# Hymba step on one Trainium2 core: weight loads issued in the order of their use

## The chip, the core and the metric

The kernel runs on one core of one Trainium2 chip. Five engines matter: TensorE (PE in the profile, its weight loads PEld), VectorE (DVE), ScalarE (ACT), GpSimd (POOL) and SyncE (SP). Each takes its instructions from its own queue, in order, and waits on semaphores for the others. SP computes nothing here: it issues every DMA of the kernel, all 1,546 of them, one behind the other, and a load whose buffer is not free holds all that stand behind it in SP's queue.

The metric is device time in microseconds of one execution. Besides the times of several runs there is one profiled execution with a trace of all instructions.

## The reference

One layer of a hybrid decoder, for 2048 prompt tokens and 32 sample tokens, in float32:

```python
def layer(x, mk, mv, s0, buf, mix_p, g_x, wq_x, wo_x, g_ffn, w_gate, w_up, conv_w, conv_b, w_down):
    m, S, sv = mixer(rmsnorm(x, mix_p[0]), s0, mix_p)
    h = x + m
    h = h + mem_attend(rmsnorm(h, g_x), mk, mv, wq_x, wo_x)
    f, new_buf = conv_ffn(rmsnorm(h, g_ffn), buf, w_gate, w_up, conv_w, conv_b, w_down)
    return h + f, S, new_buf, sv

def conv_ffn(hn, buf, w_gate, w_up, conv_w, conv_b, w_down):
    g = hn @ w_gate
    gp = jnp.concatenate([buf.astype(g.dtype), g], axis=1)
    c = conv_b + sum(conv_w[j] * gp[:, j:j + T] for j in range(CONV_W))
    return (jax.nn.gelu(c) * (hn @ w_up)) @ w_down, gp[:, -(CONV_W - 1):]
```

`mixer` is a gated linear attention (GLA) beside a chunked spatial gate (SGU), between a joint input projection `w_in` (1024 x 2576) and an output projection `w_out`; `mem_attend` is a cross attention over 256 memory tokens; `d_model` is 1024, `d_ff` 2816. The outputs are the hidden states, the states of GLA and of the convolution, the memory's keys and values, and the sample tokens' gate rows.

## The kernel before

**Arithmetic.** A float32 product is made of three PE passes: each operand is split into a part `h` (a copy rounded to the type that PE takes at full rate, by ACT, L85) and the rest `l` (DVE, L86), and `mm3` (L92 to L95) adds h·h, h·l and l·h. The large products with fixed weights go by a seven-product scheme (Strassen's form): its weight operands are three plain quarters A11, A12, A22 and four sums S1 to S4.

**Work.** The prompt goes in four blocks of 512 tokens, `s` = 0 to 3, through input projection, SGU and GLA, output projection, memory attention and FFN. The 32 sample tokens ride along: in the mixer with block 1, their memory attention (`sample_steps`, tiles `w_sq`, `kc`, `vc`) woven into the FFN of block 1, their FFN with block 2. Ahead of block 0 stand the memory's keys and values and the folding of the attention's weights. In the FFN of block 0 the weights are loaded as they are, split, and their split forms written to DRAM (`w7g`, `w7u` plain quarters, `s7g`, `s7u` sums, `wd` the split down weights); blocks 1 to 3 read these.

**Weight tiles.** Two rings in SBUF hold weights. *Raw* tiles (`rp`, 128 x 1024 float32, `NR` = 3 buffers, names `w_...`) take what must still be split. *Weight* tiles (`wp`, `NW` = 10 buffers) take what PE reads: `h_` and `l_` tiles of a split (two per raw tile), or plain tiles that come ready from DRAM. All are 512 KB. The FFN of blocks 1 to 3 takes each gate or up step (`seven_step`, eleven of either, named `wg<block><step>` and `wup<block><step>`) from five loads: A11 and A12 ready (one weight tile each), S2 with S3 raw, S1 with S4 raw (each split into two weight tiles), A22 ready. PE turns between a gate step and an up step, twelve matmuls of 256 columns on a tile quarter at a time. The `down` product reads eight ready tiles (`h_wd`, `l_wd`) for each group of four steps. In the mixer `tm_steps` loads `w_wr1` 0 to 3 as raw tiles; for block 1 some raw tiles are *held*, since the sample tokens use them unsplit (matmuls `t_wr1q`, L745).

**What sets the order.** The program is a list of `Step`s with units (their loads). `run()` walks the list and makes units ahead of their step as long as the two rings have room (`room`, L512): a unit's `load()` makes the raw load, the split and the weight tiles in one go. What the engines run is then set by a list scheduler at build time: it takes an instruction up when its operands and its buffer are free by its own timeline. Raw loads and ready loads have no order between them in this program; a raw load can be placed as soon as one of the raw buffers is free.

```python
def room(live, kind, n, size):
    return not live or made[kind] + n - live[0][0] <= size
```

Activations live in a pool `up` of `NU` = 51 tiles of 128 x 544 (`U`), with a smaller one of 8 (`T_`).

Of the kernel before, what the change touches and what calls it, by code (L numbers as in the profile page):

```python
# [9 lines left out]
F32 = mybir.dt.float32  # L10
# [27 lines left out]
def hymba_step_kernel(  # L38
# [9 lines left out]
    nc = tc.nc  # L48
# [48 lines left out]
    def W(name):  # L97
        return wp.tile([128, 1024], F32R, tag="w", name=name)

    def unit_of(load, ring=2, raws=0, held=False):  # L100
        load.ring, load.raws, load.held, load.until = ring, raws, held, None
        return load

    def raw_tile(name):
        return rp.tile([128, 1024], F32, tag="raw", name=f"w_{name}")

    def wload(w, k0, nk, m0, mw, name):
        t = raw_tile(name).rearrange("p (k m) -> p k m", k=nk)
        nc.sync.dma_start(t, w[k0 * 128:(k0 + nk) * 128, m0:m0 + mw].rearrange("(k p) m -> p k m", p=128))
        return t  # L110

    def wsplit(raw, name):

        hi, lo = (W(f"{x}_{name}").rearrange("p (k m) -> p k m", k=raw.shape[1]) for x in "hl")
        split(hi, lo, raw)
        return hi, lo

    def wunit(*spec):
        return unit_of(lambda: wsplit(wload(*spec), spec[-1]), 2, 1)

    def wraw_unit(*spec):
        return unit_of(lambda: wload(*spec), 0, 1, True)
# [12 lines left out]
    def wkeep(dst, *spec):  # L135

        def load():
            out = wsplit(wload(*spec), spec[-1])
# [3 lines left out]
        return unit_of(load, 2, 1)  # L142

# [6 lines left out]
    def seven_tile(src, name):  # L150

        def load():
            t = W(name).rearrange("p (x k m) -> p x k m", x=2, k=4)
            nc.sync.dma_start(t.bitcast(F32), src)
            return t
        return unit_of(load, 1)

# [43 lines left out]
            out[first], out[second] = (h[:, lo_], l[:, lo_]), (h[:, hi_], l[:, hi_])  # L201
        return out

    def sums_load(src, k, name):
        t = raw_tile(name)
        nc.sync.dma_start(t, src)
        return wsplit(t.rearrange("p (k m) -> p k m", k=k), name)

    def seven_step(plain, sums, get_xs, H, outs, use, name, early=False, then=None):

# [5 lines left out]
        def unit(nm):  # L216
            if nm in PLAIN:
                return seven_tile(plain[:, PLAIN.index(nm)], f"{name}{nm}")
            i = SUMS.index(nm)
            return unit_of(lambda: sums_load(sums[:, i:i + 2].rearrange("p s k m -> p (s k m)"), 8,  # L220
                                             f"{name}{nm}"), 2, 1)

        def hold(nm, w):
            if nm in PLAIN:
# [151 lines left out]
    for l in range(7):  # L376
        half = 1 << l
        n = 64 // half
# [101 lines left out]

    class Step:
        def __init__(self, fn, units=(), parts=None):
            self.fn, self.units = fn, [u if callable(u) else wunit(*u) for u in units]
            self.parts = parts or [self]

    def weave(main, *sides):
# [17 lines left out]
    def run(steps):  # L504


        steps = [p for st in steps for p in st.parts]
        index = {st: i for i, st in enumerate(steps)}
        queue = [(i, u) for i, st in enumerate(steps) for u in st.units]
        ready = {}  # L510
        ring, raws = [], []
        made = {"ring": 0, "raws": 0}  # L512
        at = 0

        def room(live, kind, n, size):
            return not live or made[kind] + n - live[0][0] <= size

        for i, st in enumerate(steps):
            now[0] = i
            flush(i - 1)  # L520
            for live in (ring, raws):
                while live and live[0][1] < i:
                    live.pop(0)
            while at < len(queue):
                j, u = queue[at]
                if not (room(ring, "ring", u.ring, NW) and room(raws, "raws", u.raws, NR)):
                    break
                until = index[u.until] if u.until else j
                if u.ring:
                    ring.append((made["ring"], j if u.held else until))  # L530
                if u.held:
                    raws.append((made["raws"], until))
                ready.setdefault(j, []).append(u())
                made["ring"] += u.ring
                made["raws"] += u.raws
                at += 1
            assert len(ready.get(i, ())) == len(st.units)
            st.fn(*ready.pop(i, []))
# [174 lines left out]
        return [(0, 272), (272, 272)] if sample else [(0, 512)]  # L713

    def wmake(w, k0, nk, m0, mw, name, dst, u):
        return unit_of(lambda: seven_make(wload(w, k0, nk, m0, mw, name), *dst, u, name), 2, 1)

    def fm_step(w, m0, get_xs, sample, evac, name, make=None):

# [15 lines left out]
    def tm_steps(w, m0, get_xs, sample, evac, name):  # L735


        ps = {}
        held = []

        def spread(j):
            if j == 1:
                ps["q"] = mps(f"t_{name}q")
            for k, raw in reversed(held):
                pe.matmul(ps["q"][hr[k % 4]], sxg[:, k * NS:(k + 1) * NS], raw, start=j == 1, stop=j == 3)  # L745
            held.clear()
            if j == 3:
                ps["t"] = T_(f"t_{name}t")
                act.activation(ps["t"][:, :512], ps["q"], AF.Copy)

        def fn(j, wu):
            xs = get_xs()
            raw, wh, wl = wu
            if sample:
                held.extend((2 * j + kk, raw[:, kk]) for kk in range(2))
                if j % 2:
                    spread(j)
            for c in range(4):
                cs = slice(c * 128, (c + 1) * 128)
                if j == 0:  # L760
                    ps[c] = acc(f"t_{name}{c}")
                for kk in range(2):
                    k = 2 * j + kk
                    mm3(ps[c], xs[k][0][:, cs], xs[k][1][:, cs], wh[:, kk], wl[:, kk], k == 0, k == 7)
                if j == 3:
                    evac(ps[c], c, 128)
            if sample and j == 3:
                ps[4] = mps(f"t_{name}4")
                pe.matmul(ps[4][:NS], sum4, ps["t"][:, :512], start=True, stop=True)
                evac(ps[4][:NS], 4, NS)  # L770

        def unit(j):
            def load():
                raw = wload(w, 2 * j, 2, m0, 512, f"{name}{j}")
                return raw, *wsplit(raw, f"{name}{j}")
            return unit_of(load, 2, 1, sample)
# [549 lines left out]
    def attention_steps(B):  # L1326
# [17 lines left out]
        def score(i, nm):  # L1344


            plain, sums = q7d[i]

            def fn(wu):
                wh, wl = wu  # L1350
                if nm == "A11":
                    B.p[i], B.ps = [None] * 4, {}
                fresh = nm in ("A11", "S1", "A12", "A22")
                if fresh:
                    B.ps[CHAIN[nm]] = acc(f"sc{s}{i}{nm}")
# [16 lines left out]
            def load():  # L1372
                return sums_load(sums[:, SUMS.index(nm)].rearrange("p k m -> p (k m)"), 4, f"qk{s}{i}{nm}")

            return Step(fn, [wready(plain[:, PLAIN.index(nm)], f"qk{s}{i}{nm}") if nm in PLAIN else unit_of(load, 2, 1)])

        def soften(i, j):

# [491 lines left out]
```

## Time and profile before

| | before |
|---|---|
| median of 3 runs | 2878.17 us (2877.86 to 2878.55) |
| profiled execution | 2877.25 us |
| its span, first to last instruction | 2875.5 us |
| mean granted clock of PE in it | 0.992 |
| moved by DMA | 592.04 MB, 205 GB/s over the span |

The page splits the span into 40 slices; each digit is a busy share in tenths, the last row the GB/s of a slice.

```profile
PE   8999999999999999999999999999999999999998
DMA  8766579999822255776885216566665324566664
GB/s 278 223 202 205 183 256 300 332 317 310 279 88 76 83 161 193 288 260 228 289 296 174 81 59 227 179 226 231 220 229 177 91 70 155 188 237 227 232 230 154
```

One slice is 71.9 us. PE is busy in all of them; the transfers are at their height in slices 7 to 11, the FFN of block 0, in which the weights are both read and written back in split form. The slices with little transfer are the mixers of blocks 1 to 3. Views used below: PE's *waits* (who waited, for which tile, total us, times, longest), *windows* (busy time and granted clock between two moments) and SP's *timeline* (when a DMA was issued). A time on SP's timeline is that of the issue; the data land later.

### The profile page before, as it was taken

To read this page: it belongs to the slowest core of one execution; us is meant where nothing else is said; L and a number is where in the kernel's file an instruction comes from. 1 tells how busy PE (TensorE), PEld (TensorE's weight loads), DVE (VectorE), ACT (ScalarE), POOL (GpSimd) and SP (SyncE) were. 2 spreads that over 40 slices of the span, in tenths; PEclk is the share of its full clock that TensorE was granted. 3 is DMA by queue.
4 is the path that set the end of the run, shared out by engine and by line. 5 is a ranking of instruction groups with operands and counts; after the bars stand their busy time and mean duration, and the time that the engine had idled before them with its cause. 6 is when DMAs were issued, how large, how long until landed. Compare 5 with 4: busy or idle time off the path is not lost.

```text
span 2875.5 us, 46693 instructions
## 1 busy us (share of the span) xinstructions
PE 2807.7 (98%) x17894; PEld 2482.3 (86%) x17894; DVE 1835.4 (64%) x3054; ACT 1216.2 (42%) x2185; POOL 562.7 (20%) x638
## 2 busy tenths in 40 slices
PE   8999999999999999999999999999999999999998
PEld 8788888888888798888888879899999888889987
DVE  6577767666747776555545777755556777654554
ACT  5545544233453354333333545533333545433333
POOL 2001212111110312222310121323221121121221
PEclk9999999999999999999999999999999999999999
DMA  8766579999822255776885216566665324566664
GB/s 278 223 202 205 183 256 300 332 317 310 279 88 76 83 161 193 288 260 228 289 296 174 81 59 227 179 226 231 220 229 177 91 70 155 188 237 227 232 230 154
DMA packets 348213, 592.04 MB, mean 206 GB/s; under 512 B 25610, under 2 KB 225388, under 8 KB 347990
## 3 DMA queue, kind: packets, MB, share of 16 engines
q1 hardware_dynamic: 347990, 589.06, 61.3%
q8 instruction: 141, 2.31, 0.3%
q14 instruction: 82, 0.67, 0.1%
HBM read 473.09 MB, written 115.87 MB: 205 GB/s over the span
## 4 chain that ended last, share of the span: by engine, by line
PE 83%; DMA 6%; DVE 5%; ACT 3%; issue 2%; POOL 1%; SPq 0%; POOLq 0%; ACTq 0%; DVEq 0%
PE d L95 6%; PE d L93 6%; PE d L94 6%; PE a_wx L95 2%; PE a_wx L94 2%; PE a_wx L93 2%; PE s L1082 2%; PE a_wg L95 1%; PE a_wup L95 1%; PE a_wup L93 1%; PE a_wg L93 1%; PE a_wg L94 1%; PE a_wup L94 1%; PE a_wu L95 1%; PE a_wu L93 1%
## 5 line engine op out<-in xcount | busy, mean ns | idle before, releaser
L93 PE MATMUL d<-acth,h_wd 128*128 128x512 f32 (+1 forms) x864 | 305.0, 354 | 0.9 <-DMA h_wd<-wd 0.9
L95 PE MATMUL d<-acth,l_wd 128*128 128x512 f32 (+1 forms) x864 | 302.6, 351 | 1.3 <-DMA l_wd<-wd 1.3
L94 PE MATMUL d<-actl,h_wd 128*128 128x512 f32 (+1 forms) x864 | 303.2, 351 | 0.0
L1719 DVE TENSOR_TENSOR h<-d,h 128x512 f32<-128x512 f32 (+1 forms) x232 | 135.0, 584 | 151.9 <-PE d L95 151.6
L95 PEld LDWEIGHTS d<-acth,l_wd 128*128 128x128 f32 x864 | 162.4, 188 | 24.1 <-DMA l_wd<-wd 2.1
L93 PEld LDWEIGHTS d<-acth,h_wd 128*128 128x128 f32 x864 | 162.4, 188 | 22.7 <-PE sop L1429 1.4
L94 PEld LDWEIGHTS d<-actl,h_wd 128*128 128x128 f32 x864 | 162.7, 188 | 20.5 <-issue 0.6
L1614 POOL TENSOR_TENSOR c<-c,bc_f 128x512 f32<-128x512 f32 (+1 forms) x88 | 128.0, 1460 | 160.8 <-ACT c L1613 159.8
L1636 POOL TENSOR_TENSOR c<-q,c 128x512 f32<-128x512 f32 (+1 forms) x33 | 48.5, 1470 | 412.7 <-DVE q L298 289.5
L1604 ACT ACTIVATE c<-g,colsb 128x512 f32<-128x512 f32 x88 | 70.7, 811 | 129.7 <-DVE g L1565 76.7
L93 PE MATMUL a_wo<-ch,h_wo 128*128 128x512 f32 (+1 forms) x320 | 115.3, 369 | 1.0 <-ACT ch L89 0.9
L94 PE MATMUL a_wo<-cl,h_wo 128*128 128x512 f32 (+1 forms) x320 | 113.3, 356 | 0.0
L95 PE MATMUL a_wo<-ch,l_wo 128*128 128x512 f32 (+1 forms) x320 | 113.1, 356 | 0.0
L85 ACT ACTIVATE acth<-c 128x512 fp32r<-128x512 f32 (+1 forms) x88 | 55.9, 637 | 121.4 <-POOL c L1636 49.5
L95 PE MATMUL a_wx<-pTh,l_wx 128*128 128x512 f32 x256 | 100.7, 394 | 0.0
L1601 POOL COPY carry<-g 128x2 f32<-128x2 f32 x88 | 36.3, 413 | 329.2 <-DVE g L1565 263.6
L94 PE MATMUL a_wx<-pTl,h_wx 128*128 128x512 f32 x256 | 100.3, 393 | 0.0
L93 PE MATMUL a_wx<-pTh,h_wx 128*128 128x512 f32 x256 | 98.8, 394 | 0.0
L86 DVE TENSOR_TENSOR actl<-c,acth 128x512 fp32r<-128x512 f32 (+1 forms) x88 | 65.0, 740 | 48.5 <-ACT acth L85 47.8
L1613 ACT ACTIVATE c<-c 128x512 f32<-128x512 f32 (+1 forms) x88 | 55.3, 636 | 78.5 <-DVE c L1606 72.3
L1605 DVE SCALAR_TENSOR_TENSOR c<-g,colsb,c 128x512 f32<-128x512 f32 x88 | 69.6, 795 | 16.3 <-ACT c L1604 16.3
L1606 DVE SCALAR_TENSOR_TENSOR c<-g,colsb,c 128x512 f32<-128x512 f32 x88 | 75.0, 856 | 1.3
(4117 smaller groups left out, 9542.5 us busy)
## 6 DMA issues: line engine op xcount, KB each, us to landing
h_wd<-wd SPq DMA_DIRECT2D x66, 512.0 KB
l_wd<-wd SPq DMA_DIRECT2D x66, 512.0 KB
w_wo<-in_w_out_dram SPq DMA_DIRECT2D x32, 512.0 KB
h_wx<-vod SPq DMA_DIRECT2D x32, 512.0 KB
l_wx<-vod SPq DMA_DIRECT2D x32, 512.0 KB
w_wg<-in_w_gate_dram SPq DMA_DIRECT2D x22, 512.0 KB
w_wup<-in_w_up_dram SPq DMA_DIRECT2D x22, 512.0 KB
w_wd<-in_w_down_dram SPq DMA_DIRECT2D x22, 512.0 KB
```

The source lines that it names most:

```text
L85: act.activation(hi, src, AF.Copy)
L86: (lo_eng or dve).tensor_tensor(lo, src, hi.bitcast(F32), ALU.subtract)
L93: pe.matmul(ps, wh, xh, start=first, stop=False, skip_group_check=again)
L94: pe.matmul(ps, wh, xl, start=False, stop=False, skip_group_check=again)
L95: pe.matmul(ps, wl, xh, start=False, stop=last, skip_group_check=again)
L1082: pe.matmul(ps3[:, :, c * 64:(c + 1) * 64], kl[:, c * 128:(c + 1) * 128], kr3[:, :, c * 64:(c + 1) * 64], start=True, stop=True)
L1604: act.activation(c[:, :SB], g[:, 2:SB + 2], AF.Identity, bias=cb, scale=w2)
L1605: dve.scalar_tensor_tensor(c[:, :SB], g[:, 1:SB + 1], w1, c[:, :SB], ALU.mult, ALU.add)
L1606: dve.scalar_tensor_tensor(c[:, :SB], g[:, 0:SB], w0, c[:, :SB], ALU.mult, ALU.add)
L1613: act.activation(c[:, :T], c[:, :T], AF.Gelu_apprx_tanh)
L1614: pool.tensor_tensor(c[:, :T], c[:, :T], B.fbc[:, :T], ALU.mult)
L1719: dve.tensor_tensor(B.h[m + mm][:, cs], ps[:, :cw], B.h[m + mm][:, cs], ALU.add)
```

## The change

A unit now has two parts: `raw`, which makes the raw load, and `make`, which splits it. `fetch()` issues every load of a weight and ties it to the one before it, so that SP issues weight loads in the order in which the program makes them (an order for the scheduler, without a semaphore). `run()` calls `fetched(done + 2)` ahead of each split: the raw tile of this split and that of the next one are loaded, no more. Raw tiles number four, at 4 KB of each partition, and activation tiles 49 instead of 51.

```diff
-NU, NT, NW, NR = 51, 8, 10, 3
+NU, NT, NW, NR = 49, 8, 10, 4
...
+    in_turn = mybir.DependencyInfo(mybir.DependencyClass.NoSync, mybir.DependencyReason.DATA)
+    before = []
+
+    def fetch(dst, src):
+        ins = nc.sync.dma_start(dst, src).ins
+        if before:
+            tc.add_manual_dep(ins, before.pop(), in_turn, reason="weights in turn")
+        before.append(ins.name)
...
-        nc.sync.dma_start(t, w[k0 * 128:(k0 + nk) * 128, m0:m0 + mw].rearrange("(k p) m -> p k m", p=128))
+        fetch(t, w[k0 * 128:(k0 + nk) * 128, m0:m0 + mw].rearrange("(k p) m -> p k m", p=128))
...
     def wunit(*spec):
-        return unit_of(lambda: wsplit(wload(*spec), spec[-1]), 2, 1)
+        return unit_of(lambda raw: wsplit(raw, spec[-1]), 2, lambda: wload(*spec))
...
-                nc.sync.dma_start(t.bitcast(F32), src[:, x])
+                fetch(t.bitcast(F32), src[:, x])
...
-        ready = {}
-        ring, raws = [], []
-        made = {"ring": 0, "raws": 0}
-        at = 0
+        raws = [(i, u) for i, u in queue if u.raw]
+        ready, ring, held, loaded = {}, [], [], {}
+        made = at = nraw = done = 0
+
+        def fetched(upto):
+            nonlocal nraw
+            while nraw < min(upto, len(raws)):
+                i, u = raws[nraw]
+                if held and nraw - held[0][0] >= NR:
+                    break
+                if u.held:
+                    held.append((nraw, index[u.until] if u.until else i))
+                loaded[id(u)] = u.raw()
+                nraw += 1
...
-                if not (room(ring, "ring", u.ring, NW) and room(raws, "raws", u.raws, NR)):
+                if ring and made + u.ring - ring[0][0] > NW:
                     break
+                if u.raw:
+                    fetched(done + 2)
+                    if id(u) not in loaded:
+                        break
+                    done += 1
...
-                ready.setdefault(j, []).append(u())
+                ready.setdefault(j, []).append(u.make(*([loaded.pop(id(u))] if u.raw else [])))
```

The other edits of the diff give each kind of unit (`wkeep`, `wmake`, `sums_load`, the units of `tm_steps` and of the query product) the same two parts. The instructions are the same in number and kind. Line numbers behind L97 shift by up to 17, and every weight load now stands at L109, in `fetch`. Three places of the order that the build gives:

SP, in the mixer of block 1, before: the loads of the weights `w_wr11` to `w_wr13`, a row of the gate's constants, stores of sample results (`svo`, `so`), two tiles of cached keys, and the output projection's first tile.

```order
L109 DMA w_wr11_9018<-in_w_in_dram 128x2x512
L109 DMA w_wr12_9024<-in_w_in_dram 128x2x512
L944 DMA gsgub_9035<-in_g_sgu_dram 32x512
L946 DMA out_8_dram<-svo_9036 32x512
L1198 DMA out_6_dram<-so00_8876 128x4x128
L1462 DMA kc000_12075<-in_cache_mem_k_dram 128x512
L1198 DMA out_6_dram<-so01_8891 128x4x128
L1462 DMA kc001_12077<-in_cache_mem_k_dram 128x512
L109 DMA w_wr13_9404<-in_w_in_dram 128x2x512
L109 DMA w_wo140_9410<-in_w_out_dram 128x4x256
```

The same place now:

```order
L109 DMA w_wr11_8741<-in_w_in_dram 128x2x512
L109 DMA w_wr12_9020<-in_w_in_dram 128x2x512
L109 DMA w_wr13_9026<-in_w_in_dram 128x2x512
L963 DMA gsgub_9037<-in_g_sgu_dram 32x512
L965 DMA out_8_dram<-svo_9038 32x512
L1217 DMA out_6_dram<-so00_8878 128x4x128
```

The load of `w_wr13` has moved six places ahead, directly behind `w_wr12`.

SP, in the FFN of block 3, around the ready tiles of gate step 8 (`wg38A11`, `wg38A12`), before:

```order
L154 DMA wup37A12_27688<-w7u7_205 128x1024
L206 DMA w_wg38S1_27907<-s7g8_208 128x1024
L206 DMA w_wup38S2_28098<-s7u8_210 128x1024
L154 DMA wup37A22_27785<-w7u7_205 128x1024
L154 DMA wg38A11_27816<-w7g8_207 128x1024
L154 DMA wg38A12_27818<-w7g8_207 128x1024
L206 DMA w_wup38S1_28132<-s7u8_210 128x1024
```

and now:

```order
L109 DMA wup37A12_27690<-w7u7_205 128x1024
L109 DMA w_wup37S1_27710<-s7u7_206 128x1024
L109 DMA w_wg38S2_27781<-s7g8_208 128x1024
L109 DMA wup37A22_27787<-w7u7_205 128x1024
L109 DMA wg38A11_27818<-w7g8_207 128x1024
L109 DMA wg38A12_27820<-w7g8_207 128x1024
L109 DMA w_wg38S1_27838<-s7g8_208 128x1024
L109 DMA w_wup38S2_27909<-s7u8_210 128x1024
```

`w_wg38S1` and `w_wup38S2` stood ahead of `wg38A11`; they now stand behind `wg38A12`. On ACT, at the same place, the splits (`h_`) and the copies of accumulators (`q`, `g`) and the convolution (`c`) before:

```order
L85 ACTIVATE h_wg38S_27838<-w_wg38S_27836 128x1024
L1604 ACTIVATE c_27802<-g_27690,colsb 128x512
L85 ACTIVATE h_wg38S_27909<-w_wg38S_27907 128x1024
L1604 ACTIVATE c_27810<-g_27692,colsb 128x512
L292 ACTIVATE q_27820<-a_wup37x 128x256
L292 ACTIVATE q_27821<-a_wup37z 128x256
```

and now:

```order
L85 ACTIVATE h_wg38S_27840<-w_wg38S_27781 128x1024
L1621 ACTIVATE c_27804<-g_27692,colsb 128x512
L1621 ACTIVATE c_27812<-g_27694,colsb 128x512
L304 ACTIVATE q_27822<-a_wup37x 128x256
L304 ACTIVATE q_27823<-a_wup37z 128x256
L304 ACTIVATE g_27944<-a_wg38x 128x256
L1630 ACTIVATE c_27804<-c_27804 128x512
L85 ACTIVATE h_wg38S_27911<-w_wg38S_27838 128x1024
```

The second split has moved behind the other rows shown.

SP, in the FFN of block 1, where the sample attention's query weights (`w_sq20`, `w_sq21`, raw and held) come between two steps, before:

```order
L206 DMA w_wup11S1_11735<-s7u1_182 128x1024
L109 DMA w_sq20_11754<-in_wq_x_dram 128x4x256
L109 DMA w_sq21_11756<-in_wq_x_dram 128x4x256
L154 DMA wup11A22_11741<-w7u1_181 128x1024
L154 DMA wg12A11_11758<-w7g2_183 128x1024
L154 DMA wg12A12_11760<-w7g2_183 128x1024
L206 DMA w_wg12S2_11778<-s7g2_184 128x1024
L206 DMA w_wg12S1_11877<-s7g2_184 128x1024
```

and now:

```order
L109 DMA w_wup11S1_11633<-s7u1_182 128x1024
L109 DMA wup11A22_11708<-w7u1_181 128x1024
L109 DMA w_sq20_11743<-in_wq_x_dram 128x4x256
L109 DMA w_sq21_11756<-in_wq_x_dram 128x4x256
L109 DMA w_wg12S2_11758<-s7g2_184 128x1024
L109 DMA wg12A11_11760<-w7g2_183 128x1024
L109 DMA wg12A12_11762<-w7g2_183 128x1024
L109 DMA w_wg12S1_11780<-s7g2_184 128x1024
```

`wup11A22` went ahead of the two sample tiles, `w_wg12S2` ahead of `wg12A11`.

More of the change, by code (lines that the diff above doesn't have):

```diff
@@ L98, in W, with unit_of @@
         return wp.tile([128, 1024], F32R, tag="w", name=name)
-    def unit_of(load, ring=2, raws=0, held=False):
-        load.ring, load.raws, load.held, load.until = ring, raws, held, None
-        return load
+    def unit_of(make, ring=2, raw=None, held=False):
+        return NS_(make=make, ring=ring, raw=raw, held=held, until=None)
+    in_turn = mybir.DependencyInfo(mybir.DependencyClass.NoSync, mybir.DependencyReason.DATA)
[5 more added lines that the diff above has]
+        before.append(ins.name)
     def raw_tile(name):
@@ L135, in wkeep, with make @@
     def wkeep(dst, *spec):
-        def load():
-            out = wsplit(wload(*spec), spec[-1])
+        def make(raw):
+            out = wsplit(raw, spec[-1])
             for x, t in enumerate(out):
@@ L141, in load @@
             return out
-        return unit_of(load, 2, 1)
+        return unit_of(make, 2, lambda: wload(*spec))
     PLAIN, SUMS = ("A11", "A12", "A22"), ("S1", "S4", "S2", "S3")
@@ L153, in load @@
             t = W(name).rearrange("p (x k m) -> p x k m", x=2, k=4)
-            nc.sync.dma_start(t.bitcast(F32), src)
+            fetch(t.bitcast(F32), src)
             return t
@@ L202, in seven_tokens, with sums_unit, raw @@
         return out
[L204 to L207, printed above, removed]
+    def sums_unit(src, k, name):
+        def raw():
+            t = raw_tile(name)
+            fetch(t, src)
+            return t.rearrange("p (k m) -> p k m", k=k)
+        return unit_of(lambda raw: wsplit(raw, name), 2, raw)
     def seven_step(plain, sums, get_xs, H, outs, use, name, early=False, then=None):
@@ L482, in __init__ @@
         def __init__(self, fn, units=(), parts=None):
-            self.fn, self.units = fn, [u if callable(u) else wunit(*u) for u in units]
+            self.fn, self.units = fn, [wunit(*u) if isinstance(u, tuple) else u for u in units]
             self.parts = parts or [self]
@@ L520, in run @@
             flush(i - 1)
-            for live in (ring, raws):
+            for live in (ring, held):
                 while live and live[0][1] < i:
@@ L525, in run @@
                 j, u = queue[at]
-                if not (room(ring, "ring", u.ring, NW) and room(raws, "raws", u.raws, NR)):
+                if ring and made + u.ring - ring[0][0] > NW:
                     break
-                until = index[u.until] if u.until else j
-                if u.ring:
-                    ring.append((made["ring"], j if u.held else until))
-                if u.held:
-                    raws.append((made["raws"], until))
-                ready.setdefault(j, []).append(u())
-                made["ring"] += u.ring
-                made["raws"] += u.raws
+                if u.raw:
[3 more added lines that the diff above has]
+                    done += 1
+                if u.ring:
+                    ring.append((made, index[u.until] if u.until and not u.held else j))
+                ready.setdefault(j, []).append(u.make(*([loaded.pop(id(u))] if u.raw else [])))
+                made += u.ring
                 at += 1
@@ L772, in unit @@
         def unit(j):
[L773 to L776, printed above, removed]
+            return unit_of(lambda raw: (raw, *wsplit(raw, f"{name}{j}")), 2,
+                           lambda: wload(w, 2 * j, 2, m0, 512, f"{name}{j}"), sample)
         out = [Step(lambda wu, j=j: fn(j, wu), [unit(j)]) for j in range(4)]
@@ L1370, in fn @@
                     soften(i, o)
-            def load():
-                return sums_load(sums[:, SUMS.index(nm)].rearrange("p k m -> p (k m)"), 4, f"qk{s}{i}{nm}")
-            return Step(fn, [wready(plain[:, PLAIN.index(nm)], f"qk{s}{i}{nm}") if nm in PLAIN else unit_of(load, 2, 1)])
+            return Step(fn, [wready(plain[:, PLAIN.index(nm)], f"qk{s}{i}{nm}") if nm in PLAIN else
+                             sums_unit(sums[:, SUMS.index(nm)].rearrange("p k m -> p (k m)"), 4, f"qk{s}{i}{nm}")])
         def soften(i, j):
```

9 lines of the change are left out of this document (3 added, 6 removed).

## The prediction

> **What bounds the kernel now.** I read the page first. Its busy line and its chain say that TensorE sets the time almost alone.
>
> ```profile
> span 2875.5 us, 46693 instructions
> PE 2807.7 (98%) x17894; PEld 2482.3 (86%) x17894; DVE 1835.4 (64%) x3054; ACT 1216.2 (42%) x2185; POOL 562.7 (20%) x638
> PE 83%; DMA 6%; DVE 5%; ACT 3%; issue 2%; POOL 1%; SPq 0%; POOLq 0%; ACTq 0%; DVEq 0%
> ```
>
> PE works for 2807.7 of 2875.5 us. The change alters no matmul, so all that an order of loads can give back lies in the other 67.8 us, and in the time that matmuls run at half clock. The second view is therefore that of PE's waits: who waited, for what, total us, times, longest. These are the waits that the change can touch, and one for a split, which gives a price below.
>
> ```profile
> PE t_wr1q L745 <- DMA w_wr<-in_w_in_dram: 4.0, 1, 4.0
> PE a_wup15x L93 <- ACT q L292: 2.6, 1, 2.6
> PE a_wg32x L93 <- DMA wg32A<-w7g: 2.5, 1, 2.5
> PE a_wg16x L93 <- DMA wg16A<-w7g: 2.3, 1, 2.3
> PE a_wg12x L93 <- DVE c L1605: 2.2, 1, 2.2
> PE a_wg38x L93 <- DMA wg38A<-w7g: 2.1, 1, 2.1
> PE a_wg310x L93 <- DVE nct L1780: 1.6, 1, 1.6
> PE mkp L93 <- ACT h_wk L85: 1.5, 1, 1.5
> PE a_wg18x L93 <- DMA wg18A<-w7g: 1.4, 1, 1.4
> PE d L95 <- DMA l_wd<-wd: 1.3, 2, 0.8
> PE a_wg34x L93 <- DMA wg34A<-w7g: 1.2, 1, 1.2
> PE d L93 <- DMA h_wd<-wd: 0.9, 1, 0.9
> ```
>
> For a_wg12x and a_wg310x the profile names the last of several semaphores; the matmuls there are the first on a plain tile, like the others, so I read them as waits for that tile (nct and c read accumulators that were done before). The waits for loads sum to 4.0+2.5+2.3+2.2+2.1+1.6+1.4+1.3+1.2+0.9 = 19.5 us, with a_wup15x, which follows wg16's delay, to 22.1.
>
> A wait also costs clock behind it. The third view is of windows: us, PE busy (matmuls), granted clock, DMA share, GB/s.
>
> ```profile
> 1330.40:1333.80 3.40, 1.12 (x10) 1.00 1.02 408
> 2542.80:2546.20 3.40, 3.40 (x18) 0.50 0.17 51
> 2546.30:2549.70 3.40, 3.40 (x31) 1.00 0.87 269
> 965.80:969.20 3.40, 3.26 (x11) 0.50 0.30 102
> 1341.30:1344.70 3.40, 3.40 (x16) 0.50 0.02 10
> 2737.30:2740.70 3.40, 3.40 (x19) 0.50 0.18 55
> ```
>
> Behind the waits of wg32 (2.5), w_wr (4.0), a_wup15x (2.6) and wg38 (2.1) the clock is 0.50 for 3.4 us, in which 1.7 us of work is lost; the neighbouring window at 1.00 holds 31 matmuls in place of 18. The window around wg16's wait (2.3) has no such drop, so a wait of two to three us brings it often, not always. In a sentence apart: the Trainium skill, "TensorE: Matmul & The Clock Gate", section "Why this matters for your kernels", asks for no idle gap over about 3 us, by which of these waits w_wr's alone would halve the clock, and the sum below would be 3.4 us smaller; the trace has drops behind 2.1 and 2.5 us, and I follow it.
>
> One more window, with all engines (PE, weight loads, DVE, ACT, POOL, then clock, DMA share and GB/s), from a stretch with the transfers at their limit:
>
> ```profile
> 504.00:576.00 72.00, 72.00 (x314) 58.59 (x313) 49.08 (x78) 21.12 (x25) 8.51 (x12) 1.00 1.03 331
> ```
>
> At 331 GB/s a tile of 512 KB takes 0.524/331 ms = **1.6 us of the queue**. SP issues every transfer, in one order, so a tile waits for all that is issued ahead.
>
> **The change part by part.** No instruction is added or removed; the order on SP changes, and with it what the scheduler does behind it.
>
> *A, w_wr13.* SP's issues (start, us, what):
>
> ```profile
> 886.23 3.57 SPq L109 DMA_DIRECT2D w_wr<-in_w_in_dram  x2
> ...
> 926.49 0.45 SPq L1462 DMA_DIRECT2D kc<-in_cache_mem_k_dram  x1
> 962.02 0.38 SPq L109 DMA_DIRECT2D w_wr<-in_w_in_dram  x1
> ```
> ```profile
> SPq L109 <- PE t_wr1q L745: 40.0, 2, 35.0
> SPq L206 <- PE sqp L1429: 19.2, 3, 10.9
> ```
>
> SP stood for 35.0 us on the load of w_wr13, since all three raw buffers were held, and PE then waited 4.0 us for it. With a fourth buffer and the load in turn, it stands directly behind w_wr12, ahead of gsgub, svo, so and kc, none of which can then hold it up. The wait and the clock behind it go: 4.0 + 1.7 = **5.7 us**. What is late next there is not a load: w_wo14's, queued behind, are asked for only after the t_wr matmuls.
>
> *B, four gate steps of block 3.* SP's issues ahead of wg32 and of wg38, and PE's first matmul on wg38:
>
> ```profile
> 2532.03 0.32 SPq L206 DMA_DIRECT2D w_wg32S<-s7g  x1
> 2532.41 0.42 SPq L154 DMA_DIRECT2D wup31A<-w7u  x1
> 2533.77 0.32 SPq L206 DMA_DIRECT2D w_wup32S<-s7u  x1
> 2534.18 1.44 SPq L154 DMA_DIRECT2D wg32A<-w7g  x2
> ```
> ```profile
> 2727.71 0.32 SPq L206 DMA_DIRECT2D w_wup38S<-s7u  x1
> 2728.13 0.87 SPq L154 DMA_DIRECT2D wup37A<-w7u  x1
> 2729.05 0.90 SPq L154 DMA_DIRECT2D wg38A<-w7g  x2
> ```
> ```profile
> 2735.92 0.36 PE L93 MATMUL a_wg38x<-w1wx,wg38A 128*128 128x256 f32 x1 [2.09 <-DMA wg38A<-w7g]
> ```
>
> wg38A11 needs 6.9 us from issue (2729.05) to first matmul, several tiles' worth: raw tiles that are not needed yet stand ahead of the plain tile that PE waits for. In the new order they stand behind A12. One raw fewer ahead gives 1.6 us, two (as at wg32, where w_wg32S1 and w_wup32S2 both went first) 3.2. That turns 2.5 (wg32), 1.6 (wg310) and 1.2 (wg34) into nothing and leaves 0.5 of wg38's 2.1. A12 then lands 1.6 us behind A11, while the twelve matmuls on A11 last 12 x 3.40/31 = 1.3 us: up to 0.3 left in each of the four. Gained: 7.4 - 0.5 - 1.2 = 5.7, and the clock behind wg32 and wg38, 3.4, as what remains is shorter than any wait with a drop: **9.1 us**.
>
> *C, block 1.* Four waits (wg12 2.2, wg16 2.3, wg18 1.4, a_wup15x 2.6) sit amid the loads of the sample attention, which go in turn as well. At wg12 the new order has two sample raws and w_wg12S2 ahead of A11, one more than before, so I count no gain there; at wg16 one raw leaves, 1.6; at wg18 1.4; a_wup15x waits for a copy on ACT and I count nothing. **3.0 us**, with bounds 0 and 8.5 plus the clock at 1341, 10.2.
>
> *D, the down tiles* h_wd and l_wd have no raw tile among them: 0, at most 2.2.
>
> *E, given back.* Raw tiles now arrive one tile or two later against their split, and ACT's order shows h of wg38's S1 five rows later, behind copies of q and g that wait for PE. Each late split costs PE its own wait.
>
> ```profile
> L85 ACT ACTIVATE h_wr<-w_wr x16: 1042/1058/1062, 205.4 to 2322.1; 128x1024 fp32r<-128x1024 f32 x16
> L86 DVE TENSOR_TENSOR l_wr<-w_wr,h_wr x16: 1204/1226/2120, 207.5 to 2323.2; 128x1024 fp32r<-128x1024 f32 x16
> ```
>
> A split takes 1.06 + 1.23 = 2.3 us. In a step PE turns to S1 after several groups of twelve matmuls of 1.3 us, mostly of the other accumulators, so it is covered where at least four groups lie between (1.6 for A12's tile, 1.6 for its own, 2.3 for the split, less 1.3 for A11's group: 4.2 us). The only place in the trace where PE shows a wait for a freshly split tile's h is mkp, 1.5 us. I take one such wait for each of the three FFN blocks: **-4.5 us**. Bounds: nothing (a split that comes later gains nothing by itself), and one for each of the six steps of B and C that ran late, with two clock drops: 6 x 1.5 + 3.4 = 12.4.
>
> *F, everything else that moves.* The early stage (memory keys, folded weights, block 0's split and store of weights) has its stores and reads of DRAM forms stand elsewhere among the loads, and there are two activation tiles fewer. No row of PE's waits is one for an activation tile. I take 0; both ways the bound is one place like A, 5.7 us.
>
> Sum: -5.7 - 9.1 - 3.0 + 4.5 = **-13.3 us** against the profiled execution, whose own time is 2877.25 us (1.75 around its span). The median of the runs is 2878.17, 0.92 above it. 2878.17 - 13.3 = **2864.9 us**.
>
> **The rivals.**
>
> *The wait moves.* The bytes and the ring of ten weight tiles are the same, so what A11 gains, S1's split loses: E at its upper bound, 12.4, and C at 0. Then 2878.17 - 5.7 - 9.1 + 12.4 = 2875.8, no change. For it: ACT's order, where the split moved behind dependent copies. Against it: PE has two chains, gate and up, to turn between, and no raw of these steps shows a wait on PE today.
>
> *The queue in turn stops.* Slower. In block 1 the raw tiles of the sample queries (w_sq) are held until their matmuls; SP's row above has three such waits behind sqp, 19.2 us, 10.9 the longest. Before, a raw load that could not start was placed late by the scheduler, with plain tiles ahead of it. In turn, the FFN's plain tiles stand behind it. A stop decides only where it outlasts what PE has in its ten weight tiles, the cover that turned w_wr13's 35.0 us into 4.0. Without any cover three stops cost 19.2 and three drops 5.1, 24.3 in all: 2878.17 - 5.7 - 9.1 - 3.0 + 4.5 + 24.3 = 2889.2. For it: w_sq20 and w_sq21 now stand ahead of wg12's tiles with w_wg12S2. Against it: four raw buffers in place of three, so fewer of these waits at all.
>
> *It gives everything.* No split is late and block 1 gains its 10.2: 5.7 + 9.1 + 10.2 = 25.0, 2853.2.
>
> *It does nothing.* If the waits for plain tiles came from the weight buffers coming free and not from the queue, A11 would land as before, and only A counted: 2872.5 before what is given back, 2877 with it. Against it: at 2729.05 the issue stood open 6.9 us before the matmul, which is queue and not buffer.
>
> **How the numbers follow.** Chances: forecast 0.48, everything 0.15, the wait moves or nothing is done 0.21, the stop 0.16. Measurements of this kernel tell about 0.2% (5.8 us) from no change, so faster means under 2872.4 and slower over 2883.9. Faster: 0.48 + 0.15 = 0.63, less 0.03 for a forecast with F against it, plus 0.02 of the third: 0.62. Slower: the stop at 0.16 and 0.01 for F on top of the third: 0.17. Same: 0.21. The range takes in everything with F's bound half on top (2850) and the stop without cover (2889). Cases of one sign hold most of the chance; the forecast's own range is 2856 to 2872.
>
> **What would show it.** In the new profile the row t_wr1q <- w_wr should be gone and SP should show no 35 us on it (A). Rows a_wg32x, a_wg34x, a_wg310x should be gone and a_wg38x under 1 us, with clock 1.00 behind them (B). The load of wg38A11 should come 1.6 us sooner after its issue; if it is still 6.9, the queue was not the cause. New rows with ACT h or DVE l of S tiles, or a copy q, as releaser would be E. Long SP waits on sqp or on splits in block 1 with PE waiting at the plain tiles of wg12 to wg19 would be the stop. New waits in the first 250 us, on q7, kr, rowsb or an activation tile, would be F, and would make me wrong without touching B's reading.

## The result, and the profile after

| | before | after |
|---|---|---|
| median (lowest to highest) | 2878.55 us (2877.86 to 2889.54, 5 runs) | 2860.63 us (2856.59 to 2865.12, 5 runs) |
| ratio, 95% interval | | 0.9925 [0.9903, 0.9947] |
| profiled execution | 2877.25 us | 2856.59 us |

The change makes the kernel 17.9 us faster; 13.3 were forecast. The profiled execution is the fastest of its five, so the traces differ by more than the medians: 20.6 us of span.

The page of the changed kernel, the same three lines as before:

```profile
span 2854.9 us, 46641 instructions
PE 2803.4 (98%) x17894; PEld 2476.6 (87%) x17894; DVE 1844.4 (65%) x3054; ACT 1215.6 (43%) x2185; POOL 576.0 (20%) x638
PE 84%; DMA 5%; DVE 5%; ACT 2%; issue 1%; POOL 1%; SPq 0%; POOLq 0%; ACTq 0%; DVEq 0%
```

The counts by engine are those of before; the 52 instructions fewer in the total are waits on semaphores. PE's busy time fell by 4.3 us with the same matmuls, and the mean granted clock is 0.995 (before it was 0.992). Counting the stretches of 3.4 us at clock 0.50 in each trace, without the first and last ones, gives twelve before and six after: 6 x 1.7 = 10.2 us less lost to half speed. This is not simply a share of the 20.6. PE's idle time fell by 16.3 us (67.8 to 51.5) and its busy time by only 4.3, so the matmuls outside those stretches took some 6 us more than before; why is not shown. Some of PE's waits of the changed kernel, for weights, for their splits and for copies that free an accumulator:

```profile
PE a_wup15x L93 <- ACT q L304: 3.1, 1, 3.1
PE a_wg36x L93 <- DMA wg36A<-w7g: 1.5, 1, 1.5
PE a_wg16z L93 <- DVE g L310: 1.2, 1, 1.2
PE a_wg16z L95 <- DVE l_wg16S L86: 1.2, 1, 1.2
PE a_wup32z L93 <- ACT q L304: 0.9, 1, 0.9
PE a_wg34x L93 <- DMA wg34A<-w7g: 0.7, 1, 0.7
PE colpsb L423 <- DMA rowsb<-in_g_sgu_dram: 0.6, 1, 0.6
PE a_wg310x L93 <- DMA wg310A<-w7g: 0.5, 1, 0.5
PE a_wg32x L93 <- DMA wg32A<-w7g: 0.5, 1, 0.5
PE a_wg38x L93 <- DMA wg38A<-w7g: 0.5, 1, 0.5
```

The row t_wr1q <- w_wr is gone, and block 3's plain tiles are waited for by half a microsecond each; wg36, which no wait stood on before, has 1.5. In block 1's FFN (the names with `wg1`, `wup1`) the waits have moved: wg16's first matmul waits no longer, but its second quarter waits for an addition on DVE (g) and then for a split, and the wait for the copy of wup15 still stands.

To see *where* the time came from, I compare the start of the same matmul in two traces. The first matmul on wg38 started at 2735.92 before; here it is after:

```profile
2717.89 0.36 PE L93 MATMUL a_wg38x<-w1wx,wg38A 128*128 128x256 f32 x1 [0.45 <-DMA wg38A<-w7g]
```

That is 18.0 us sooner. The median of this difference over the matmuls around the end of a stage, less the same at the end of the stage before, is what the stage gained. This table of **stages** serves all the experiments below (us against the kernel before, each from one trace; negative is sooner). The stages end at 420, 820, 1110, 1540, 2490 and 2845 us of the trace before.

| trace | to 420: memory, folding, first mixer | block 0 FFN | block 1 mixer | block 1 FFN | block 2, mixer 3 | block 3 FFN | sum |
|---|---|---|---|---|---|---|---|
| the change | -12.1 | +0.3 | -5.4 | +2.6 | +0.8 | -6.9 | -20.8 |
| e7, the same again | -8.1 | +0.3 | -3.5 | +3.7 | -1.9 | -3.9 | -13.3 |
| e1, four raw buffers alone | -9.1 | -0.8 | -5.6 | -1.3 | +1.2 | -2.8 | -18.4 |
| e2, in turn, three buffers | +0.4 | -0.1 | +2.5 | +6.4 | +0.6 | -3.6 | +6.1 |
| e3, no raw ahead | -10.2 | +0.3 | -5.3 | +9.1 | +1.3 | -4.5 | -9.3 |
| e4, two raw ahead | -10.6 | -0.9 | -5.7 | +7.0 | -1.2 | -4.6 | -15.9 |
| e5, block 1's FFN free | -9.9 | +0.3 | -5.5 | -1.9 | +0.9 | -7.7 | -23.7 |
| e6, only it in turn | -9.3 | -0.9 | -4.5 | +2.5 | +2.2 | -6.0 | -16.1 |
| e8, 49 tiles alone | -2.6 | -2.6 | +1.8 | +2.1 | +2.0 | -1.0 | -0.4 |

Rows one and two are the same program, and their entries differ by up to 4 us, so a single entry below that says nothing. Of the 4.0 in the first column, 3.4 are the two clock drops that e7 has there and the first trace has not; the 3.0 in block 3 are no drop. The largest entry of the change stands in the first column, where I had forecast 0.

### The profile page after: what moved, and what is told of

The parts are those of the page before. It is cut to its first block, busy times and chain, and to the rows that moved or that the text cites. A ratio compares the mean times of both kernels' runs of the same rounds, so it can differ in the third digit from the quotient of the medians.

```text
span 2854.9 us, 46641 instructions
## 1 busy us (share of the span) xinstructions
PE 2803.4 (98%) x17894; PEld 2476.6 (87%) x17894; DVE 1844.4 (65%) x3054; ACT 1215.6 (43%) x2185; POOL 576.0 (20%) x638
## 4 chain that ended last, share of the span: by engine, by line
PE 84%; DMA 5%; DVE 5%; ACT 2%; issue 1%; POOL 1%; SPq 0%; POOLq 0%; ACTq 0%; DVEq 0%
PE d L95 6%; PE d L94 6%; PE d L93 6%; PE a_wx L93 2%; PE a_wx L95 2%; PE a_wx L94 2%; PE s L1101 2%; PE a_wg L93 1%; PE a_wg L95 1%; PE a_wup L93 1%; PE a_wup L95 1%; PE a_wg L94 1%; PE a_wup L94 1%; PE a_wo L93 1%; PE a_wu L93 1%
## 5 line engine op out<-in xcount | busy, mean ns | idle before, releaser
L1618 POOL COPY carry<-g 128x2 f32<-128x2 f32 x88 | 42.9, 492 | 324.4 <-DVE g L1582 276.0
```

## The experiments

The change has two parts that can be had apart: a fourth raw buffer (paid for with two activation tiles), and loads in turn with raw tiles one ahead. **Theory 1** after the result: the buffer gave the first and third columns, the order the last. **Theory 2**: the order gave it all, and the buffer only made room for it. The first four kernels ran on one chip, beside the kernel before (2881.3 us there).

**e1, four raw buffers in the kernel before.**

```diff
-NU, NT, NW, NR = 51, 8, 10, 3
+NU, NT, NW, NR = 49, 8, 10, 4
```

> The kernel before with four raw buffers and 49 activation tiles, and nothing else of the change. Theory 1 (two separate gains): the fourth buffer alone gives what came in the first 360 us (-12 us in the profiled pair) and in the mixer of block 1 (-5.6, the wait on w_wr13 gone), while block 3 keeps its waits for wg32, wg34, wg38 and wg310, which grow, as a fourth raw tile can now go ahead of the plain ones (1.6 us each): -17.6 + 0 to +6, so 2861 to 2867 us. Theory 2 (the order gives everything, the buffer only makes room for it): 2876 to 2880 us, and the early stage is as it was.

Measured: 2860.33 us, ratio 0.9927 [0.9912, 0.9941]. Without any change to the order of issue by hand the kernel gains what the whole change gains. Of its waits:

```profile
PE a_wg16x L93 <- DMA wg16A<-w7g: 2.1, 1, 2.1
PE a_wg38x L93 <- DMA wg38A<-w7g: 2.0, 1, 2.0
PE a_wg310x L93 <- DMA wg310A<-w7g: 1.6, 1, 1.6
PE a_wg32x L93 <- DVE l_wg32S L86: 1.1, 1, 1.1
PE a_wg34x L93 <- DMA wg34A<-w7g: 1.1, 1, 1.1
PE a_wg36x L93 <- DMA wg36A<-w7g: 0.9, 1, 0.9
PE colpsb L411 <- DMA rowsb<-in_g_sgu_dram: 0.4, 1, 0.4
```

w_wr is gone from the list, colpsb is down from 2.5, and block 3's waits are still there: 2.0 + 1.6 + 1.1 + 1.1 + 0.9 = 6.7 us on the five even gate steps, 3.7 in the changed kernel. They did not grow by 1.6 as I had expected, although w_wup38S1 too goes ahead of wg38A11 in this build: a place in the queue is not always paid in full.

**e2, the order without the buffer.** The same line of the changed kernel set back to 51 and 3.

> The changed kernel with three raw buffers and 51 activation tiles: the loads in turn alone. Theory 1: the first 360 us and w_wr13's wait of 4 us stay as before; block 3's waits for plain tiles shrink to about 0.5 us each (-6.8 us) and block 1's FFN loses 2 to 3: 2871 to 2876 us. Theory 2: at least -14 us, 2860 to 2865 us.

Measured: 2880.25 us, ratio 0.9997 [0.9988, 1.0007]: nothing. Theory 2 falls, and theory 1 had the order worth more than it is.

```profile
PE t_wr1q L766 <- DMA w_wr<-in_w_in_dram: 4.1, 1, 4.1
PE colpsb L423 <- DMA rowsb<-in_g_sgu_dram: 2.5, 1, 2.5
PE a_wg38x L93 <- DMA wg38A<-w7g: 2.0, 1, 2.0
PE a_wg16z L95 <- DVE l_wg16S L86: 1.4, 1, 1.4
PE a_wup110z L95 <- DVE l_wup110S L86: 1.3, 1, 1.3
```

The two waits that e1 removed are whole. Block 3 gains 3.6 us by its stage, and block 1's FFN loses 6.4, part of it in waits for splits (the last two rows), which the kernel before does not have. The row of wg38 matters too: SP issues the loads there in the changed kernel's order, and PE still waits 2.0 us, with 6.4 us from the issue of wg38A11 to its first use.

**e3 and e4, raw tiles none and two ahead of their split**, in the changed kernel:

```diff
-                    fetched(done + 2)
+                    fetched(done + 1)    # e3; done + 3 in e4
```

> The changed kernel with each raw tile loaded only when its own split comes up (none ahead). If what is left of the waits for plain tiles in block 3 (0.5 to 1.5 us at five steps) comes from the raw tile ahead of them in the queue, these go (-3 us); if the cover of the splits is what the one raw tile ahead buys, waits with the h or l split of an S tile as releaser come up in blocks 1 to 3, over 1 us each. I expect the first to be smaller than the second: 2860 to 2868 us.

Measured: 2869.82 us, ratio 0.9959 [0.9944, 0.9974].

```profile
PE a_wup19z L95 <- DVE l_wup19S L86: 2.1, 1, 2.1
PE a_wg16z L95 <- DVE l_wg16S L86: 1.7, 1, 1.7
```

The waits for splits came up, almost all in block 1, where the stage loses 9.1. In block 3 the waits on the five gate steps did shrink, from 3.7 to 1.6 us, as the first of the two expectations has it, but waits for the convolution's carry (ncp) came up to 3.6 us, and the stage does not gain on the changed kernel. wg38 still waits 0.5 in it, with no raw tile between A22 and A11: what is left there is not a raw tile's place.

> The changed kernel with raw tiles loaded two ahead of their split. One raw tile more stands ahead of A11 in each step: if a place in the queue is worth 1.6 us, the waits for wg32, wg34, wg36, wg38 and wg310 in block 3 grow by 1.6 each from 0.5 to 1.5 (+8 us with none of it covered), and the wait for the split of wg16's S1 in block 1 (1.2 us) goes: 2863 to 2869 us. If the plain tiles wait for their weight buffers rather than for the queue, block 3 stays as it is with one ahead: 2859 to 2861 us.

Measured: 2860.97 us, ratio 0.9928 [0.9914, 0.9943]: the time of the second answer, but not block 3 as it was. wg38 and wg310 wait 1.1 each instead of 0.5, not the 1.6 more of the first, and wg34 and wg36 do not grow; the split of wg16 is waited for no longer, and another load is, with the stage of block 1 at +7.0:

```profile
PE d L93 <- DMA h_wd<-wd: 5.1, 2, 3.3
PE a_wup15x L93 <- ACT q L304: 3.3, 1, 3.3
```

**e5 and e6, the chain by stage.** The stage table says that the order gives in block 3 and takes in block 1's FFN. In e5 the loads of block 1's FFN, with the sample attention woven into it, are left out of the chain; in e6 only they are in it. On SP, e5 has the changed kernel's order outside that stretch and e1's within it, e6 the reverse.

```diff
+    turn, apart = [True], []
     def fetch(dst, src):
         ins = nc.sync.dma_start(dst, src).ins
+        if not turn[0]:
+            return
...
+                turn[0] = steps[j] not in apart      # e6: in apart
                 ready.setdefault(j, []).append(u.make(...))
...
+            apart += [p for st in fmain + smp_steps for p in st.parts]
```

> The changed kernel with the loads of block 1's FFN and of the sample attention woven into it left out of the chain; all other loads stay in turn, four raw buffers. On SP its order is that of the changed kernel outside this stretch and that of e1_four_raw within it. If the gains and losses of the order are local to their stage, the traces so far give -3.9 us against the changed kernel (block 1's FFN cost it 2.6 against the kernel before, and e1_four_raw gained 1.3 there), and block 3 keeps its -6.9: 2855 to 2858 us. If they are not (the stages trade with each other, or it is where the clock drops fall), 2859 to 2862 us.

> The opposite: four raw buffers, and the chain only for the loads of block 1's FFN and the sample attention in it. Local gains and losses give e1_four_raw's 2860.3 us and 3.9 more: 2863 to 2866 us, with block 3 as in e1_four_raw (-2.8 against before). If not local, 2859 to 2862 us.

> The changed kernel once more, beside the two above on their chip, to see how far its stages repeat in a second trace: about 2860.6 us; the stages of the first trace (-12.1 up to block 0's FFN, -5.4 in the mixer of block 1, +2.6 in block 1's FFN, -6.9 in block 3) should come again except for 1.7 us for each drop of the clock that comes or goes.

Measured on one chip (before 2882.42 us there): e5 2858.0 us, ratio 0.9920 [0.9903, 0.9938]; e6 2861.75, 0.9940 [0.9922, 0.9957]; e7, the changed kernel again, 2863.93, 0.9940 [0.9924, 0.9955]. e5's six runs (2853.55 to 2860.67) and e7's six (2860.47 to 2866.99) hardly touch: leaving block 1 out is worth 5.9 us by the medians, and it keeps the gain of block 3. These are e5's waits on the five gate steps there:

```profile
PE a_wg36x L93 <- DMA wg36A<-w7g: 1.2, 1, 1.2
PE a_wg310x L93 <- DMA wg310A<-w7g: 0.5, 1, 0.5
PE a_wg34x L93 <- DMA wg34A<-w7g: 0.5, 1, 0.5
PE a_wg38x L93 <- DMA wg38A<-w7g: 0.4, 1, 0.4
```

2.6 us in place of e1's 6.7. e6 is better than I expected: by the medians it has -20.7 us against its own before, e1 -21.0, and the intervals of their ratios overlap, so in time it shows no loss, although its stage has the +2.5 of block 1. Its block 3 has -6.0 where e1 has -2.8, with the same order of weight loads around the five gate steps: the same order gave both. The stages are local in e5; in e6 that is not settled.

**e8, the two activation tiles.** The kernel before with `NU` = 49 and three raw buffers.

> The kernel before with 49 activation tiles and still three raw buffers: the price of the two tiles alone. If the tiles cost nothing, as no wait for one shows, 2878 to 2882 us, and the first 360 us as before; if part of the early gain came from the different order that fewer tiles give, the first 360 us are shorter by some of the 9 to 12 us; if the missing tiles hold something up, up to 6 us more.

Measured: 2879.81 us, ratio 0.9994 [0.9981, 1.0006]. The tiles alone neither cost nor give anything that shows. Its first stage has -2.6; two of the three clock drops of that stage are missing in its trace, which is 3.4 us by itself, and the wait on colpsb is 2.3 against 2.5. The early gain is the buffer's.

**e9 to e12, is block 1's loss the order's?** The sample attention's steps are spread over more or fewer steps of the FFN, in the changed kernel and in e5:

```diff
-            sides.append((sample_steps(), 1, len(fmain) - 5))
+            sides.append((sample_steps(), 1, len(fmain) - 4))    # e9, e10; - 7 in e11, e12
```

> The changed kernel with the sample attention's steps spread over one more step of block 1's FFN, so that loads, softmax and copies meet the FFN elsewhere. If what block 1's FFN loses in turn (2.6 and 3.7 us in two traces) comes from the one order of loads, it comes again: 2860 to 2865 us, and 3 to 6 more than e10_free_sample_later. If it was chance, the copy of wup15 that stands 3.1 us behind the sample's softmax on ACT, that wait goes and the two are within 2 us of each other.

> e5_block1_free with the same later sample steps: block 1's FFN free of the chain. Order theory: 2855 to 2860 us, 3 to 6 below e9_in_turn_sample_later. Chance theory: within 2 us of it.

> The changed kernel with the sample attention's steps spread over two steps fewer. Order theory: 3 to 6 us more than e12_free_sample_earlier. Chance theory: within 2 us of it.

> e5_block1_free with the same earlier sample steps. Order theory: 3 to 6 us below e11_in_turn_sample_earlier. Chance theory: within 2 us of it.

| | sample steps | median | ratio, 95% interval | block 1 FFN by stage | block 3 FFN |
|---|---|---|---|---|---|
| e9, in turn | later | 2857.74 us | 0.9913 [0.9898, 0.9928] | -0.4 | -8.6 |
| e10, free | later | 2854.36 us | 0.9904 [0.9889, 0.9919] | -0.8 | -5.0 |
| e11, in turn | earlier | 2855.83 us | 0.9913 [0.9892, 0.9934] | -1.8 | +0.1 |
| e12, free | earlier | 2857.56 us | 0.9917 [0.9894, 0.9941] | -3.9 | -8.3 |

(Before: 2883.81 us on this chip.) In turn against free is +3.4 us in one pair, which is what the order theory expected, and -1.7 in the other, which is what chance expected; with four runs each the intervals of both pairs overlap. The stage says more: block 1 in turn loses nothing against before in either pair, and in turn against free it costs 0.4 and 2.1 us there, where it was 4.5 and 5.6 (the change and e7 against e5). So most of that loss comes from this order together with these sample steps, and not from the order as such; a smaller price is not excluded. The largest single wait in block 1's FFN is part of it. ACT in the changed kernel (start, us, line, what):

```profile
1322.71 1.28 ACT L1517 ACT_TABLE_LOAD   x1 [1.21 <-DVE smx L1516]
...
1324.57 0.37 ACT L304 ACTIVATE q<-a_wup15x 128x256 f32<-128x256 f32 x1
```

and in e9:

```profile
1317.98 0.36 ACT L304 ACTIVATE q<-a_wup15x 128x256 f32<-128x256 f32 x1
...
1321.95 1.28 ACT L1517 ACT_TABLE_LOAD   x1 [1.21 <-DVE smx L1516]
```

The copy q that frees PE's accumulator stood behind the sample's softmax with its table load; in e9 it stands ahead of it, and the 3.1 us wait is not in e9's list. But the place on ACT is not the whole cause. The copy stands behind the softmax in the kernel before, in e1 and in e5 too, with waits of 2.6, 0.2 and 0.4 us; in e1 and e5 PE had stood 2.1 and 2.2 us for wg16A11 shortly before, and the change has no such wait. So against the kernel before the wait for q is only 0.5 us of the loss, and against e5 part of it seems to be a wait that has moved.

Of the versions tried, e10 has the lowest median against its own before (-29.5 us, where the change has -17.9 and -18.5), followed by e11, e12 and e9 within 4 us. They did not run beside the changed kernel; e5 did, and it beats both kernels on one chip.

## Why the prediction was right, and where it was not

The direction was right, the time (2864.9 for 2860.63) inside the forecast's own range. The reasons were right in part of the terms, and that the time came out so near is luck: without the first stage, where I had forecast 0, the stages of the first trace sum to -8.7 us in place of -13.3.

**A, w_wr13, -5.7: right.** The stage gave -5.4 (-3.5 in e7), and e1 gives -5.6 with the buffer alone, e2 the whole 4.1 us wait with the order alone. So the buffer does it and the order has no part. One sign I had named was wrong: SP still stands there for 36.8 us.

```profile
915.68 0.45 SPq L1479 DMA_DIRECT2D kc<-in_cache_mem_k_dram  x1
952.98 11.64 SPq L109 DMA_DIRECT2D w_wo<-in_w_out_dram  x8
```

With one buffer more it is the next raw tile, w_wo's, that waits behind the held ones, and PE does not need it yet. A long wait on a queue says nothing until one asks who needs what stands in it.

**B, block 3, -9.1: right in this trace, not in all, and too large.** wg38A11 was issued at 2713.07 and first used at 2717.89, 4.8 us later in place of 6.9, and 0.5 of wg38's wait remains, both about as worked out:

```profile
2713.07 0.80 SPq L109 DMA_DIRECT2D wg38A<-w7g  x2
```

The named waits went from 7.4 to 2.2 us (0.5 + 0.5 + 0.5 + 0.7), and both clock drops are gone. What the sum missed is wg36's new 1.5 and wup32's 0.9; the stage gave -6.9, and -3.9 in e7.

How much of that is the order's is not settled by one trace. The eight traces with this order, one raw tile ahead (the change, e2, e5, e7, e9 to e12), have 2.5 to 6.4 us of waits on the five even gate steps, 4.4 on average. The four with the order before (before, e1, e6, e8) have 4.8 to 8.5, 6.8 on average. So the order is worth some 2.4 us of waits, with ranges that overlap. In e11 wg38 waits 2.2 us and the stage gains nothing (+0.1), with the order of the changed kernel; as in e2, its A11 is in use 6.4 to 6.5 us after its issue, not far from the 6.9 that I had named as the sign against the queue. That e3, with no raw tile ahead, has 1.6 us speaks for the place in the queue as one cause of these waits; what else sets them stays open.

**C, block 1's FFN, -3.0: wrong, also in sign.** It gave +2.6 and +3.7. The wait of wg16's first matmul did go. At its second quarter, which starts at 1316.25, PE then waits 1.2 us, and not for a load: the one semaphore there is DVE's, whose addition g reads an accumulator and stood behind the split of the first raw tile (S2):

```profile
1313.58 2.01 DVE L86 TENSOR_TENSOR l_wg16S<-w_wg16S,h_wg16S 128x1024 fp32r<-128x1024 f32 x1 [1.12 <-PE a_wg15x L94]
1315.51 0.68 DVE L310 TENSOR_TENSOR g<-a_wg15x,g 128x512 f32<-128x512 f32 x1
```

The other 1.2 us, at 1319.45, are for the split of S1 itself. The copy of wup15, which I had read as following wg16's delay, still makes PE wait when that delay is gone. e9 to e12 show that most of the loss goes with the place of the sample's steps.

**D, the down tiles, 0: right.** h_wd has 0.9 us before and after; l_wd's 1.3 is not in the first trace, and 0.7 of it is in e7.

**E, late splits, +4.5: seen, smaller.** There is one such row, l_wg16S with 1.2 us, and the 1.2 us of the addition behind a split is another of its kind. e2 and e3 have more of them (1.3 to 2.1), so the price per wait was right, and how often it falls due changes with the buffers and with how far ahead the raw tiles go.

**F, everything else, 0: the step that failed.** "I take 0; both ways the bound is one place like A, 5.7 us." The first 420 us gave -12.1 and -8.1. The waits of the trace before that went are small ones, for a load of constants and for folding the query weights:

```profile
PE qkp L93 <- ACT wqh L85: 1.7, 1, 1.7
PE s L1082 <- ACT qkf L659: 0.9, 1, 0.9
PE mkt L615 <- DVE mkf L606: 0.5, 2, 0.3
PE t_ws L93 <- ACT xh L89: 0.5, 1, 0.5
```

With colpsb's 2.5 to 0.6 they make 1.9 + 1.7 + 0.9 + 0.5 + 0.5 = 5.5 us. The rest is clock: before, three windows of this stage hold a drop (0.96 is 3.4 us at half speed in 40),

```profile
40.00:80.00 40.00, 36.88 (x294) 0.96 0.90 301
80.00:120.00 40.00, 36.55 (x204) 0.96 0.59 187
280.00:320.00 40.00, 37.26 (x172) 0.96 0.59 196
```

and after none of them does:

```profile
40.00:80.00 40.00, 39.34 (x312) 1.00 0.87 300
80.00:120.00 40.00, 38.25 (x222) 1.00 0.79 247
280.00:320.00 40.00, 37.32 (x170) 1.00 0.47 154
```

3 x 1.7 = 5.1 us; 10.6 of the 12.1 are in rows. I had looked in this stage for waits that carry the name of a weight that the change could touch, and found none; but with three buffers raw tiles arrive later there, and what that costs stands under other names. The raw tiles of the query weights, `w_wqf`, show it. These are their eight loads, with the first and last issue, before and in e1:

```profile
L109 SPq DMA_DIRECT2D w_wqf<-in_wq_x_dram x8: 372/388/938, 56.4 to 148.7; - x8
L109 SPq DMA_DIRECT2D w_wqf<-in_wq_x_dram x8: 368/384/449, 51.4 to 129.4; - x8
```

The last one is issued between 146.6 and 149.1 us in every trace with three buffers (before, e2, e8), and between 128.7 and 131.9 in every one with four. wqh and qkf, for which qkp and s wait in the list above, are made from these tiles; the wait of s is 0.9 to 1.0 us in all three traces with three buffers and is in none with four (in four of those the matmul bp waits 0.4 to 0.7 us for qkf instead). That it is the buffer is shown by e1, e2 and e8; the way through `w_wqf` is read from the traces for these two waits, and was not tried apart.

**The rivals.** "It does nothing" and "the wait moves" had the order right: alone, in e2, it gains nothing, and by the stages what it gains in block 3 it loses in block 1. "The queue in turn stops" did not come as described: no wait on sqp is left on SP with four buffers, and in e2, with three, they sum to 13.3 us in place of 19.2. Waits on the sample's cache tiles grew there, that on kTp from 24.6 to 41.9 us; whether they hold up a tile that PE needs was not tried. "It gives everything" did not come either: block 1's FFN gained nothing. The time was within the forecast's range because an unforeseen term of -12 stood in for terms that fell short.

## What to carry to other kernels

When a change brings a buffer and an order together, forecast the two apart and build each alone: here the buffer is the whole gain (0.9927 alone) and the order nothing that shows (0.9997 alone). A shortage of buffers costs time in stages where no wait is named after them; count in which stages the pool is full, not only where PE waits for a load by name. An order that helps in one stage can cost where other work is woven in (leaving block 1 out gave 5.9 us): tie it only where more than one trace of that stage shows a gain.

## What the runs showed of the hardware

Short waits on PE cost clock as well: beside 16.3 us less of idle time the changed kernel's trace has six stretches of 3.4 us at half clock fewer, 10.2 us of lost work. Where they fall is not fixed: around 290 us, where the same short waits on otp stand in each (1.8 and 0.4 us), the changed kernel's first trace has no drop (1.00 above) and its second, e7, a double one:

```profile
280.00:320.00 40.00, 37.63 (x160) 0.91 0.43 140
```

Nor is it the clock alone: e7 has six drops like the first trace and a span 7.5 us longer (2862.4), with longer waits for the same tiles, wg310 1.6 us in place of 0.5 and wg34 1.1 in place of 0.7. The changed kernel's five runs spread over 8.5 us, those of the kernel before over 11.7; one trace is not enough to price a stage. By the Trainium skill, "TensorE: Matmul & The Clock Gate", section "What's actually happening", the window that decides is free-running; that two traces of one program place their drops differently agrees with it.
